# Feed-forward by block products: issuing the B11 + B12 difference behind the splits of the three-block sum

## The chip, the cores and the metric

The kernel runs on one core of a Trainium2 chip. The metric is the device time of one execution in microseconds (us), as the median of three timed runs. A separate execution was profiled; every duration, start and wait below is from that one.

## What is computed

One layer of a hybrid block on 256 tokens of width 2048, in float32. The part that matters here is the gated feed-forward behind the mixer:

```python
h2 = rms_norm(x, g_ffn)
gate, up = jnp.split(h2 @ w_ffn_in, 2, axis=-1)
x = x + (jax.nn.silu(gate) * up) @ w_ffn_out
```

`w_ffn_in` is 2048 x 11264 and `w_ffn_out` 5632 x 2048.

## The kernel before

**Precision.** TensorE multiplies in fp32r. A weight tile is therefore split in two: ScalarE casts it to `hi` (`whi`, L733), VectorE subtracts to get `lo = w - hi` (`wlo`, L734), and a product is three passes: hi by hi, hi by the lo part of the activations, lo by hi. TensorE can start on a piece when its `whi` is there, and needs its `wlo` after two thirds of the piece (12 matmuls: eight with `whi`, then four with `wlo`).

**The first feed-forward product** is done by groups. There are 22; each has 2 x 128 columns of gate and up, and its 2 x 2 blocks B11, B12, B21, B22 stand in four raw tiles of 128 x 2048. Groups 0 and 1 are multiplied plainly. Groups 2 to 21 use seven block products in place of eight; some of their weights are sums of blocks, and these are made in place:

- B12 + B22: a GpSimd transfer that adds into the tile `x` (L769).
- the three-block sum: `q2` on VectorE, `x = x + b11` (L877).
- B11 + B12: `q1` on VectorE, `b11 = x - b22` (L891).
- the sum with B21: `q4`, a GpSimd transfer that adds `x` into the tile `b21` (L888).

**A cycle** is one group's worth of work. Its products, in the order of the code, are (two pieces each): the next group's pair is already prepared ahead, then C with `x`; B with the three-block sum, whose pieces are called x0 and x1 below; A with `b21` (b21-0, b21-1); B with B11 + B12 (b11-0, b11-1); the next group's first product; B with `b22`; C with the summed `b21`. Between them stand pieces D of the second product (`w_ffn_out`), two in a cycle of groups 3 to 5 and four from group 6 on, and the transposes of the activations.

**Order.** `run` goes through the list of pieces; the split of piece n is written ahead of the products of piece n - 3 (`LOOK = 3`), and each product is followed by what reads its bank. `q2` is written ahead of x0's split and `q1` ahead of b11-0's. A planner then issues, on each engine, the ready instruction that stands first in the code; an instruction written later can be issued earlier when nothing ahead of it is ready. There are four `whi` and four `wlo` buffers, so splits run at most four pieces ahead of TensorE.

The steps that the prediction speaks of on VectorE are, beside L734, L877 and L891: L956 (adds a D piece's result to the residual), L881, L895, L897, L900, L904 (banks read), L805 (gating), L933 (the lo part of the transposed activations; its hi part is L932 on ScalarE).

Of the kernel before, what the change touches and what calls it, by code (L numbers as in the profile page):

```python
# [7 lines left out]
F32 = mybir.dt.float32  # L8
# [38 lines left out]
def block_kernel(ctx: ExitStack, tc: tile.TileContext, xT, vec,  # L47
                 wvf, wqk, wxy, wpi, wgate, wri, wpool, wbr, wout, wffi, wffo, out):
    nc = tc.nc
    V, S, G, PE = nc.vector, nc.scalar, nc.gpsimd, nc.tensor  # L50
# [37 lines left out]
    def split(r, a, n, V=V, S=S):  # L88

        hi = hl_p.tile([P, RAW // 2], F32R, name="whi")  # L90
        lo = hl_p.tile([P, RAW // 2], F32R, name="wlo")
        with tc.high_priority(offset=AHEAD):
            S.copy(hi[:, :n], r[:, a:a + n])  # L93
            V.tensor_sub(lo[:, :n], r[:, a:a + n], hi[:, :n].bitcast(F32))  # L94
        return hi, lo
# [207 lines left out]
    def split_w(k):  # L303
        return split(raws[k // 2], k % 2 * W3, W3, Vo, So)
# [14 lines left out]
    for k in range(EARLY):  # L319
# [7 lines left out]
        else:  # L327
            w = split_w(k)
# [13 lines left out]
    w = ahead  # L342
# [12 lines left out]
    for k in range(EARLY, KD):  # L355
# [13 lines left out]
        w = ahead  # L369
# [31 lines left out]
    def scores(h, q, k):  # L401

        sc = aux()
        for t in range(2):
            n = (t + 1) * P
            o = sc[:, off[t]:off[t] + n]
            tq = slice(t * P, (t + 1) * P)
            tl = slice(T + t * P, T + (t + 1) * P)
            PE.matmul(o, lhsT=q[:, tq], rhs=k[:, :n], start=True, stop=False)
            PE.matmul(o, lhsT=q[:, tq], rhs=k[:, T:T + n], start=False, stop=False)  # L410
            PE.matmul(o, lhsT=q[:, tl], rhs=k[:, :n], start=False, stop=False)
            PE.matmul(o, lhsT=LF[:, h, tq], rhs=RF[:, h, :n], start=False, stop=True)
        ns = at_p.tile([P, 3 * P], F32, name="ns")
        st = at_p.tile([P, 8], F32, name="st")
        ph = at_p.tile([P, 3 * P], F32R, name="ph")
        pl = at_p.tile([P, 3 * P], F32R, name="pl")
        for t in range(2):
            c = slice(off[t], off[t] + (t + 1) * P)
            V.tensor_tensor_reduce(out=ns[:, c], in0=sc[:, c], in1=mask[:, c], scale=-1.0,
                                   scalar=3e38, op0=ALU.add, op1=ALU.min, accum_out=st[:, t:t + 1])  # L420
            S.activation(ns[:, c], ns[:, c], AF.Exp, bias=st[:, t:t + 1], scale=-1.0,
                         accum_out=st[:, 2 + t:3 + t])
        V.reciprocal(st[:, 4:6], st[:, 2:4])
        for t in range(2):
            c = slice(off[t], off[t] + (t + 1) * P)
            S.activation(ph[:, c], ns[:, c], AF.Copy, scale=st[:, 4 + t:5 + t])
            V.scalar_tensor_tensor(pl[:, c], ns[:, c], st[:, 4 + t:5 + t], ph[:, c].bitcast(F32),
                                   ALU.mult, ALU.subtract)
        return ph, pl
# [47 lines left out]
    for h in range(H):  # L477
# [3 lines left out]
        p = scores(h, q, k)  # L481
# [157 lines left out]
    for m in range(KD):  # L639
# [3 lines left out]
        for b, y in enumerate((yB, yC, yA)):  # L643
            hi, lo = split(r3, b * 1024, 1024) if b < 2 else split(r1, 0, 1024)
# [70 lines left out]
    line, todo = [], []  # L715

    def fill():

        while raws and todo:
            w = todo.pop(0)  # L720
            w.tile = raws.pop(0)
            w.load(w.tile)

    def split_piece(p, ahead):
        for f in p.pre:
            f()
        hi = hl_p.tile([P, RAW // 2], F32R, name="whi")[:, :1024]
        lo = hl_p.tile([P, RAW // 2], F32R, name="wlo")[:, :1024]
        w = p.src()
        if len(w.shape) == 3:  # L730
            hi, lo = halves(hi), halves(lo)
        with tc.high_priority(offset=ahead):
            S.copy(hi, w)  # L733
            V.tensor_sub(lo, w, hi.bitcast(F32))  # L734
        for f in p.done:
            f()
        for w in p.uses:
            w.uses -= 1
            if not w.uses:
                raws.append(w.tile)  # L740
        fill()
        p.parts = hi, lo
# [12 lines left out]
    def halves(r):  # L755
        return r.rearrange("p (j c) -> p j c", j=2)
# [28 lines left out]
    def product(g, w, form, c, start, pre=None, done=None, post=None, more=()):  # L785

        for h in range(2):
            def mm(hi, lo, h=h):
                o = g.place(c)
                for part, v in ((0, hi), (1, hi), (0, lo)):  # L790
                    for j in range(4):
                        PE.matmul(o, lhsT=hs[:, 4 * h + j, form, part, :], rhs=v[:, :, j * P:(j + 1) * P],  # L792
                                  start=start and h == 0 and part == 0 and v is hi and j == 0,
                                  stop=h == 1 and v is lo and j == 3, skip_group_check=True)

            Piece(lambda h=h: halves(w.tile)[:, :, h * 512:(h + 1) * 512], mm, [w, *more],
                  [pre] if pre and h == 0 else [], [done] if done and h else [],
                  [post] if post and h else [])

    def tmp(nm):  # L800
        return ft_p.tile([P, T], F32, name=nm)

    def gated(t, a, up, g):

        V.scalar_tensor_tensor(a, up, r2[:, t:t + 1], g, ALU.mult, ALU.mult)  # L805
# [4 lines left out]
    def first(g):  # L810
        if g.i in PLAIN:
            both(g, g.b11, (("C", 4, True), ("A", 0, True)), lambda: less(g, "t0", "A", "C"))
        else:
            product(g, g.b11, 0, "A", True, post=lambda: copy(g, "m1", "A"))
# [59 lines left out]
    def group(g, nxt, slot, mid):  # L874

        def q2():
            V.tensor_add(g.x.tile, g.x.tile, g.b11.tile)  # L877

        def d():
            g.d = sm.tile([P, T], F32, name="t0")  # L880
            V.tensor_sub(g.d, g.m1, g.bank["B"])  # L881

        def silu0():
            g.g0 = sm.tile([P, T], F32, name="t1")
            S.activation(g.g0, g.bank["A"], AF.Silu, scale=r2[:, 0:1])

        def q4():
            G.dma_start(g.b21.tile, g.x.tile, accum_op=ALU.add)  # L888

        def q1():  # L890
            V.tensor_sub(g.b11.tile, g.x.tile, g.b22.tile)  # L891

        def s():
            s_ = sm.tile([P, T], F32, name="evt")
            V.tensor_sub(s_, g.bank["B"], g.m1)  # L895
            g.u1 = tmp("u1")
            V.tensor_sub(g.u1, s_, g.bank["C"])  # L897

        def up0():
            V.tensor_sub(g.m1, g.bank["B"], g.m1)  # L900
            gated(0, g.m1, g.m1, g.g0)

        def end():
            V.tensor_add(g.d, g.d, g.bank["C"])  # L904
            S.activation(g.d, g.d, AF.Silu, scale=r2[:, 1:2])
            gated(1, g.u1, g.u1, g.d)

        product(g, g.x, 4, "C", True)
        slot(0)

        product(g, g.x, 5, "B", True, pre=q2, post=d, more=[g.b11])
        mid()
        product(g, g.b21, 1, "A", False, done=q4, post=silu0, more=[g.x])
        slot(1)
        product(g, g.b11, 3, "B", False, pre=q1, post=s, more=[g.x, g.b22])
        if nxt is not None:
            first(nxt)
        slot(2)
        product(g, g.b22, 6, "B", False, post=up0)
        product(g, g.b21, 2, "C", False, post=end)  # L920
        slot(3)

    def turn(g, c, f):

        if f == 0:
            acts[c] = act_p.tile([P, 2 * max(CHUNKS), 2 * T], F32R, name="act")
        act = acts[c]
        tp = aux_p.tile([P, 2, T], F32, name="turn")
        for j in range(2):
            for t, a in enumerate((g.m1, g.u1)):  # L930
                PE.transpose(tp[:, j, t * P:(t + 1) * P], a[:, j * P:(j + 1) * P], ident.bitcast(F32))  # L931
        S.copy(act[:, f:f + 2, :T], tp)  # L932
        V.tensor_sub(act[:, f:f + 2, T:], tp, act[:, f:f + 2, :T].bitcast(F32))  # L933
# [42 lines left out]
    def behind(f):  # L976

        line[-1].post.append(f)
# [14 lines left out]
    for i, (c, at) in enumerate(owner):  # L993
        g, prev = nxt, (g if i else None)
        nxt = Group(i + 1) if i + 1 < len(owner) else None

        def slot(k):
            if nxt is None and k == 3:
                return
            for _ in range(SLOTS[c][k]):  # L1000
                if queue:
                    queue.pop(0)()

        def mid():
            if prev is None:
                behind(stats)
                return
            pc, pat = owner[i - 1]
            behind(lambda a=(prev, pc, 2 * pat): turn(*a))
            if pc != c:  # L1010
                queue.extend(down(pc))

        (plain if i in PLAIN else group)(g, nxt, slot, mid)
# [145 lines left out]
```

## Time and profile before

| | |
|---|---|
| median of three timed runs | 1528.62 us (1528.33 to 1530.21) |
| the profiled execution's own time | 1532.99 us |
| its span, first to last instruction | 1531.0 us |
| TensorE matmul busy | 1508.2 us, 99% |
| TensorE weight loads busy | 1411.3 us, 92% |
| VectorE busy | 1205.4 us, 79% |
| ScalarE busy | 923.8 us, 60% |
| mean granted TensorE clock | 0.997 |

The span begins and ends with the program's instructions; the execution's own time is 1.99 us longer. The shares are means over the whole kernel; the feed-forward begins near 820 us, and there VectorE is busier than 79%.

### The profile page before, as it was taken

The numbers are of one execution on the slowest core, as the hardware profiler recorded it, in microseconds if no ns is written. First come the engines' busy times: TensorE is split into PE (matmuls) and PEld (weight loads), VectorE is DVE, ScalarE is ACT, GpSimd is POOL, SyncE is SP. The second block draws the span as 40 slices with busy tenths as digits, with TensorE's granted clock in tenths as the row PEclk, the third lists the DMA queues.
The fourth block names the chain that finished last, engine by engine and source line by source line (L and its number), as shares of the span: only waits on it lengthen the run. The fifth ranks groups of instructions, "written<-read, shape, count | busy, mean of one in ns | idle before, by whom it ended". The sixth has DMA issues, their size and how long they took to land.

```text
span 1531.0 us, 26475 instructions
## 1 busy us (share of the span) xinstructions
PE 1508.2 (99%) x10628; PEld 1411.3 (92%) x10628; DVE 1205.4 (79%) x1593; ACT 923.8 (60%) x1319; POOL 119.5 (8%) x170
## 2 busy tenths in 40 slices
PE   9999999999999999999999999999999999999996
PEld 8988888888888888888889999999999999999996
DVE  7866677788565656567796999999889998999974
ACT  6766567666454444455675666566565665656663
POOL 1000011202000000000110010010000000000012
PEclk9999999999999999999999999999999999999998
DMA  7644455555555554656757699878889888887851
GB/s 259 212 165 150 135 192 185 200 173 206 189 183 199 172 207 165 206 170 234 264 187 219 197 254 277 286 228 252 258 275 295 243 249 267 281 278 242 238 204 55
DMA packets 70858, 331.09 MB, mean 216 GB/s; under 512 B 5584, under 2 KB 6480, under 8 KB 52816
## 3 DMA queue, kind: packets, MB, share of 16 engines
q1 hardware_dynamic: 61840, 286.54, 52.3%
q0 software_dynamic: 8320, 41.95, 14.5%
q8 instruction: 83, 1.36, 0.3%
q10 hardware_dynamic: 576, 0.92, 0.2%
q14 instruction: 39, 0.32, 0.1%
HBM read 306.32 MB, written 2.10 MB: 201 GB/s over the span
## 4 chain that ended last, share of the span: by engine, by line
PE 90%; DVE 4%; DMA 2%; issue 1%; ACT 1%; POOL 0%; SPq 0%; POOLq 0%; DVEq 0%; ACTq 0%
PE acc L106 30%; PE bank L792 23%; PE acc L107 15%; PE obank L117 5%; PE obank L116 5%; PE obank L115 5%; PE bank L834 3%; DVE wlo L734 2%; DMA raw<-raw 2%; PE acc L72 1%; PE aux L72 1%; PE turn L931 1%; DMA raw<-in_wvf 1%; DVE wlo L72 0%; POOL lev L580 0%
## 5 line engine op out<-in xcount | busy, mean ns | idle before, releaser
L733 ACT CAST whi<-raw 128x1024 fp32r<-128x1024 f32 x384 | 393.9, 1050 | 226.9 <-PE obank L116 57.5
L734 DVE TENSOR_TENSOR wlo<-raw,whi 128x1024 fp32r<-128x1024 f32 x384 | 456.4, 1220 | 61.5 <-ACT whi L733 59.0
L106 PE MATMUL acc<-hT,whi 128*128 128x512 f32 x1392 | 489.7, 395 | 0.0
L94 DVE TENSOR_TENSOR wlo<-raw,whi 128x1024 fp32r<-128x1024 f32 (+1 forms) x262 | 320.2, 1222 | 188.9 <-ACT whi L93 188.2
L93 ACT CAST whi<-raw 128x1024 fp32r<-128x1024 f32 (+1 forms) x262 | 270.2, 1032 | 208.5 <-PE acc L106 181.6
L107 PE MATMUL acc<-hT,wlo 128*128 128x256 f32 x1392 | 390.7, 281 | 0.0
L106 PEld LDWEIGHTS acc<-hT,whi 128*128 128x128 f32 x1392 | 261.6, 188 | 59.4
L792 PE MATMUL bank<-whi,hs 128*128 128x256 f32 x2240 | 312.6, 281 | 1.5 <-ACT whi L733 1.5
L792 PEld LDWEIGHTS bank<-whi,hs 128*128 128x128 f32 x2240 | 284.0, 188 | 2.4 <-ACT whi L733 2.1
L107 PEld LDWEIGHTS acc<-hT,wlo 128*128 128x128 f32 x1392 | 262.4, 189 | 0.0
L115 PE MATMUL obank<-act,whi 128*128 128x256 f32 x704 | 197.5, 281 | 0.0
L116 PE MATMUL obank<-act,whi 128*128 128x256 f32 x704 | 197.4, 280 | 0.0
L117 PE MATMUL obank<-act,wlo 128*128 128x256 f32 x704 | 197.3, 281 | 0.0
L792 PE MATMUL bank<-wlo,hs 128*128 128x256 f32 x1120 | 179.1, 282 | 4.6 <-DVE wlo L734 4.4
L792 PEld LDWEIGHTS bank<-wlo,hs 128*128 128x128 f32 x1120 | 151.9, 188 | 7.1 <-DVE wlo L734 6.7
L116 PEld LDWEIGHTS obank<-act,whi 128*128 128x128 f32 x704 | 132.6, 188 | 0.0
L115 PEld LDWEIGHTS obank<-act,whi 128*128 128x128 f32 x704 | 132.4, 188 | 0.0
L117 PEld LDWEIGHTS obank<-act,wlo 128*128 128x128 f32 x704 | 132.3, 188 | 0.1
L106 PE MATMUL acc<-mT,whi 128*128 128x512 f32 x256 | 89.6, 394 | 0.0
L107 PE MATMUL acc<-mT,wlo 128*128 128x256 f32 x256 | 71.5, 280 | 0.0
L769 POOL DMA_DIRECT2D raw<-in_wffi x20 | 24.2, 1210 | 514.7 <-DVE wlo L734 262.6
L106 PEld LDWEIGHTS acc<-mT,whi 128*128 128x128 f32 x256 | 48.1, 188 | 11.2 <-DVE mT L655 0.2
(288 smaller groups left out, 1766.9 us busy)
## 6 DMA issues: line engine op xcount, KB each, us to landing
raw<-in_wffi SPq DMA_DIRECT2D x88, 1024.0 KB, 7.3
raw<-in_wgate SPq DMA_DIRECT2D x48, 1024.0 KB, 4.9
raw<-in_wffo SPq DMA_DIRECT2D x44, 1024.0 KB, 8.6
raw<-in_wffi POOLq DMA_DIRECT2D x20, 1024.0 KB, 8.3
raw<-raw POOLq DMA_DIRECT2D x20, 1024.0 KB, 11.4
raw<-in_wqk SPq DMA_DIRECT2D x16, 1024.0 KB, 4.8
raw<-in_wxy SPq DMA_DIRECT2D x16, 1024.0 KB, 4.9
raw<-in_wbr SPq DMA_DIRECT2D x16, 1024.0 KB, 5.0
```

Source lines behind the costliest of these rows:

```text
L72: self.last = f(*args, **kw)
L93: S.copy(hi[:, :n], r[:, a:a + n])
L94: V.tensor_sub(lo[:, :n], r[:, a:a + n], hi[:, :n].bitcast(F32))
L106: PE.matmul(ps, lhsT=hi[:, w], rhs=rhs(k), start=first and k == 0, stop=False)
L107: PE.matmul(ps[:, :T], lhsT=lo[:, w], rhs=rhs(k)[:, :T], start=False, stop=last and k == nk - 1)
L115: PE.matmul(o, lhsT=hi[:, w], rhs=rhs(k)[:, :T], start=first and k == 0, stop=False)
L116: PE.matmul(o, lhsT=hi[:, w], rhs=rhs(k)[:, T:], start=False, stop=False)
L117: PE.matmul(o, lhsT=lo[:, w], rhs=rhs(k)[:, :T], start=False, stop=last and k == nk - 1)
L733: S.copy(hi, w)
L734: V.tensor_sub(lo, w, hi.bitcast(F32))
L792: PE.matmul(o, lhsT=hs[:, 4 * h + j, form, part, :], rhs=v[:, :, j * P:(j + 1) * P], start=start and h == 0 and part == 0 and v is hi and ...
L834: PE.matmul(o, lhsT=hs[:, 4 * h + j, form, part, :], rhs=v[:, :, j * P:(j + 1) * P], start=start and h == 0 and part == 0 and v is hi and ...
```

## The change

`q1`, the subtraction that makes B11 + B12, gets an order edge: it may not be issued on VectorE before the second `wlo` split of the three-block sum (x1's) has been issued. The edge orders issue alone; it adds no wait for a result. Nothing else is added or removed, and no instruction changes its operands.

```diff
         with tc.high_priority(offset=ahead):
             S.copy(hi, w)
-            V.tensor_sub(lo, w, hi.bitcast(F32))
+            p.sub = V.tensor_sub(lo, w, hi.bitcast(F32))
...
         def q1():
-            V.tensor_sub(g.b11.tile, g.x.tile, g.b22.tile)
+            with tc.issue_after(g.sums.sub.ins):
+                V.tensor_sub(g.b11.tile, g.x.tile, g.b22.tile)
...
         product(g, g.x, 5, "B", True, pre=q2, post=d, more=[g.b11])
+        g.sums = line[-1]
         mid()
```

## Rows read from the trace of the kernel before

**Rows 1.** Waits of TensorE's weight loads, 980 to 1470 us, then 850 to 980.

```profile
PEld bank L792 <- DVE wlo L734: 6.1, 8, 1.5
...
PEld bank L792 <- ACT whi L733: 2.1, 3, 0.8
PEld bank L792 <- DVE wlo L734: 0.6, 3, 0.2
```

**Rows 2.** Waits of TensorE's matmuls over the whole span: total us, times, longest.

```profile
PE bank L792 <- DVE wlo L734: 4.4, 6, 1.3
```

**Rows 3.** VectorE in order of time, group 10: start, us, instruction, count.

```profile
1088.45 2.28 DVE L877 TENSOR_TENSOR raw<-raw,raw 128x2048 f32<-128x2048 f32 x1
1090.65 0.41 DVE L956 TENSOR_TENSOR xt<-xt,obank 128x256 f32<-128x256 f32 x1
1090.98 2.28 DVE L891 TENSOR_TENSOR raw<-raw 128x2048 f32<-128x2048 f32 x1
1093.19 3.49 DVE L734 TENSOR_TENSOR wlo<-raw,whi 128x1024 fp32r<-128x1024 f32 x3
1096.60 0.41 DVE L956 TENSOR_TENSOR xt<-xt,obank 128x256 f32<-128x256 f32 x1
1096.93 2.35 DVE L734 TENSOR_TENSOR wlo<-raw,whi 128x1024 fp32r<-128x1024 f32 x2
1099.20 0.41 DVE L881 TENSOR_TENSOR t<-m,bank 128x256 f32<-128x256 f32 x1
1099.53 0.68 DVE L933 TENSOR_TENSOR act<-turn,act 128x512 fp32r<-128x512 f32 x1
1100.13 1.22 DVE L734 TENSOR_TENSOR wlo<-raw,whi 128x1024 fp32r<-128x1024 f32 x1
```

**Rows 4.** ScalarE in the same stretch, with the idle time before each.

```profile
1090.85 4.84 ACT L733 CAST whi<-raw 128x1024 fp32r<-128x1024 f32 x5 [3.30 <-DVE raw L877]
1096.17 1.05 ACT L733 CAST whi<-raw 128x1024 fp32r<-128x1024 f32 x1 [0.48 <-PE bank L792]
```

**Rows 5.** TensorE's weight loads in the same stretch: x0, x1 and b11-0.

```profile
1091.95 1.00 PEld L792 LDWEIGHTS bank<-whi,hs 128*128 128x128 f32 x8
1094.46 0.54 PEld L792 LDWEIGHTS bank<-wlo,hs 128*128 128x128 f32 x4 [1.50 <-DVE wlo L734]
1094.92 1.01 PEld L792 LDWEIGHTS bank<-whi,hs 128*128 128x128 f32 x8
1095.86 0.55 PEld L792 LDWEIGHTS bank<-wlo,hs 128*128 128x128 f32 x4
...
1102.47 1.00 PEld L792 LDWEIGHTS bank<-whi,hs 128*128 128x128 f32 x8
```

**Rows 6.** Group 10's transfer q4, and the cast and split that wait for it.

```profile
1098.45 0.90 POOL L888 DMA_DIRECT2D raw<-raw  x1 [1.56 <-DVE wlo L734]
...
1111.40 1.05 ACT L733 CAST whi<-raw 128x1024 fp32r<-128x1024 f32 x1 [3.80 <-DMA raw<-raw]
...
1112.48 1.23 DVE L734 TENSOR_TENSOR wlo<-raw,whi 128x1024 fp32r<-128x1024 f32 x1 [3.33 <-ACT whi L733]
```

**Rows 7.** The same VectorE idle time in groups 14 and 19.

```profile
1239.43 1.22 DVE L734 TENSOR_TENSOR wlo<-raw,whi 128x1024 fp32r<-128x1024 f32 x1 [0.54 <-ACT whi L733]
...
1399.41 1.23 DVE L734 TENSOR_TENSOR wlo<-raw,whi 128x1024 fp32r<-128x1024 f32 x1 [3.80 <-ACT whi L733]
```

**Rows 8.** Cycles: window, length, then busy us (count) of PE, PEld, DVE, ACT, POOL.

```profile
878.28:905.23 26.95, 26.95 (x228) 26.76 (x228) 26.95 (x32) 17.87 (x20) 2.09 (x2) 1.00 0.92 258
905.23:932.30 27.07, 26.64 (x221) 26.07 (x220) 27.04 (x31) 17.93 (x20) 2.09 (x2) 1.00 0.94 273
932.30:959.48 27.18, 26.71 (x223) 26.19 (x222) 27.04 (x32) 17.87 (x20) 2.09 (x2) 1.00 0.94 272
1088.45:1121.09 32.64, 31.34 (x266) 31.14 (x265) 29.31 (x34) 19.72 (x22) 2.10 (x2) 1.00 0.84 253
1214.99:1246.55 31.56, 31.56 (x270) 31.56 (x269) 29.58 (x33) 20.30 (x22) 2.10 (x2) 1.00 0.91 283
```

**Rows 9.** VectorE in order of time in an early cycle, group 4.

```profile
905.23 2.29 DVE L877 TENSOR_TENSOR raw<-raw,raw 128x2048 f32<-128x2048 f32 x1
907.43 0.48 DVE L805 SCALAR_TENSOR_TENSOR u<-u,r,t 128x256 f32<-128x256 f32 x1
907.95 0.42 DVE L956 TENSOR_TENSOR xt<-xt,obank 128x256 f32<-128x256 f32 x1
908.28 2.28 DVE L891 TENSOR_TENSOR raw<-raw,raw 128x2048 f32<-128x2048 f32 x1
```

**Rows 10.** VectorE around b11-0's split in group 13, and TensorE's start on b11-0.

```profile
1195.11 1.22 DVE L734 TENSOR_TENSOR wlo<-raw,whi 128x1024 fp32r<-128x1024 f32 x1
...
1198.20 0.54 PEld L792 LDWEIGHTS bank<-whi,hs 128*128 128x128 f32 x4
```

## The prediction

> **What bounds the kernel now.** I read the page first: TensorE is busy 99% of the span, so a change on VectorE can only win back what TensorE loses by waiting. Next the waits of TensorE, to see how much that is and for whom. In the feed-forward they are few: 980 to 1470 us holds eight waits of the weight loads for a `wlo`, 6.1 us together, and 850 to 980 holds three more of 0.6 and three for a `whi` of 2.1 [rows 1]. That is 8.8 us in all, 0.58% of the span. The matmuls' own waits give less, 4.4 us where the loads give 6.7 [rows 1, 2]. I go by the loads: in group 10 eight loads of x0 begin at 1091.95 and the next four at 1094.46, 2.51 later, where x1 takes 0.94 for the same step [rows 5]; the difference of 1.57 is what the loads' row calls 1.50. The Trainium skill says the same (Perfetto Trace Analysis, Identifying the Most-Contended Engine): matmul busy time is a poor measure of TensorE's headroom and the loads' busy share a good one; by the matmuls the ceiling would be 4.4 + 1.5 = 5.9 us, and this trace sides with the loads.
>
> Then VectorE in order of time beside ScalarE, to see why x0's `wlo` is late. In group 10, `q2` ends at 1090.73, an L956 follows, then `q1` holds VectorE from 1090.98, and x0's `wlo` starts at 1093.19, the instant VectorE is free [rows 3]. ScalarE had x0's `whi` ready at 1090.85 + 1.05 = 1091.90 [rows 4]. So `q1` stands in the way.
>
> Last, whole cycles, for VectorE's room. It differs by stage: 27.04 busy of 27.07 and 27.04 of 27.18 in groups 4 and 5, 26.95 of 26.95 in group 3, but 29.58 of 31.56 in group 14 [rows 8]. In three early cycles VectorE, not TensorE, sets the pace (loads busy 26.07 of 27.07); the fifteen late ones have some 2 us of room each.
>
> **Part 1: `q1` leaves its place.** Without it x0's `wlo` can start 0.04 behind its `whi` (the distance of 1112.45 to 1112.48 elsewhere [rows 6], rounded up), at 1091.94 instead of 1093.19: 1.25 us earlier. Of the 1.50 wait 0.25 stays, and every wait under 1.25 at this place goes. Each of the eight late ones is at x0, the longest 1.5 [rows 1]: at most some 6.1 - 2 x 0.25 = 5.6 back from them by this step alone. The next splits move up with it.
>
> **Part 2: where `q1` goes.** The edge names x1's `wlo`, but the planner decides. VectorE's order behind `q1` is that of the code: x0, x1, b21-0, L956, b21-1, D, L881, L933, b11-0 [rows 3]. Only `q1` stands out of its turn: its place in the code is right in front of b11-0, and it was drawn forward while x0's `whi` was not ready. With the edge there is such a hole behind x1 only if b21-0's `whi` is late, and ScalarE casts five pieces in 4.84 us, 0.95 each [rows 4], against some 1.14 a split (3.49 for three, which overlap by 0.08). So I expect b21-0 first, and `q1` at its written place, behind L933.
>
> **Part 3: what waits for `q1` there.** Behind it on ScalarE's queue stands b11-0's cast, which ran at 1096.17 [rows 4] and must now wait; behind that cast, b11-1's and the next group's. In group 10, `q1` begins at 1100.13 - 1.25 = 1098.88 [rows 3] and ends 2.28 later, 1101.16; the cast starts 0.12 later (as 1090.73 to 1090.85) and is done at 1102.33, 2.20 behind the old start of b11-0's `wlo`. TensorE reached b11-0 at 1102.47 [rows 5], 2.34 behind the same start, but now comes earlier by what it got back at x0, here 1.25. So 1.11 of the 1.25 is lost again. By the same steps every late cycle keeps only 0.14 of its gain: eight cycles, 8 x 0.14 = 1.1 us. This is the lower bound of the late gain. A cycle without a wait has cover: in group 13 the cast is done at 1195.11 + 2.20 = 1197.31, and TensorE arrives at 1198.20 [rows 10].
>
> **Part 4: what else moves up.** `q4` is issued 0.3 behind b21-1's `wlo` (the first of the two at 1096.93, over at 1098.15 [rows 3, 6]). That split runs 1.25 earlier, so the transfer does too. In group 10 its landing is what starts ScalarE again at 1111.40 after 3.80 idle, and VectorE after 3.33 [rows 6]; from there VectorE runs nearly without pause into the next `q2`. VectorE now reaches this point 2.24 later (1102.37 against 1100.13 at b11-0), so of 3.33 idle 1.09 is left for the earlier landing to use: the next cycle starts 1.1 earlier, and that covers a loss of up to 1.1 at its b11-0. The idle time here goes from 0.54 to 3.80 [rows 7], so some cycles gain all and some nothing. Of the 6.1 - 1.1 = 5.0 that part 3 takes back, I let 1.6 stand, nearer to the row of group 10 than to that of group 14, because the long waits come in cycles that follow a long idle time. Late gain: 6.1 - 1.6 = 4.5, between 1.1 and 6.1 (an earlier cycle start also takes the last 0.25 at x0).
>
> **Part 5: the early cycles pay.** The change puts two holes into VectorE's order where none was: between `q2` and x0's `wlo` (0.12 + 1.05 + 0.04 = 1.21) and between `q1` and b11-0's (1.21 again). In groups 3 to 5 VectorE has no idle time, so what is not filled lengthens the cycle. Fillers are there: an L805 (0.40 of spacing) and an L956 (0.33) run between `q2` and `q1` now [rows 9] and leave 0.48 of the first hole; the second can take one or two L956 of the D pieces, 0.33 each, which leaves 0.55 to 0.88. Together 1.0 to 1.4; taking 1.0 for three cycles, 3.0, and 0.1 for group 6, which has some room behind: 3.1. The bounds are 0 (everything filled) and 2 x 1.21 x 4 = 9.7. The 2.7 of waits that these cycles show now [rows 1] is TensorE waiting for a VectorE that is full; it is no separate gain. The page cited above counts VectorE's occupancy as a fair measure of its room, which agrees with 27.04 of 27.07; by that rule every hole left open there is paid in full.
>
> **Sum.** -4.5 + 3.1 = -1.4 us. From the profiled span of 1531.0 that gives 1529.6, and of the execution's 1532.99, 1531.6. That execution is 4.4 above the median of the timed runs; the change acts alike on both, so 1528.62 - 1.4, about **1527.2 us**.
>
> **Rivals.** *Clearly faster, 0.34.* Fillers close most of the early holes (cost 1.0, not 3.1), and the earlier `q4` covers b11-0 everywhere: -6.0 + 1.0 = -5.0, 1523.6. For it: L956 wait nearby in each early cycle, and the long late idle times; against it: the 0.54 of group 14. *Slower by the early holes, 0.12.* In groups 3 to 6 neither hole is filled, 9.7, and the late gain of 4.5 stands: +5.2, 1533.8. It decides from 4.5 / 4 = 1.1 us of open hole a cycle on. Against it: the two fillers of rows 9 are ready at that place. *Slower by `q1` right behind x1, 0.11.* If the planner sees b21-0's `whi` late, `q1` takes the place the edge names. Then VectorE idles 1.21 - 0.33 = 0.88 before x0, and all from b21-0 on comes 0.9 to 1.0 later than now: the old wait moves from x0 to b21-0, D's split is late too, and `q4` is issued 0.9 later, which carries into the next cycle. Some 10 of 19 cycles would pay 0.9: +9, 1537.6. For it: the five casts are only 0.19 a piece ahead of VectorE; against it: they are ahead. *No effect.* That the order stays as it was is excluded in the cycles shown, since `q1` stands ahead of x0 in them; that all cancels is inside the forecast.
>
> **How the numbers follow.** The forecast has 0.43, its own range 1524.5 to 1530.5. A change of 0.2%, 3.1 us, is about what a measurement of this kernel can tell from none: under 1525.6 is faster, above 1531.7 slower. Faster: 0.34 and a little of the forecast, 0.36; slower: 0.12 + 0.11 = 0.23; same: 0.41. The range for 8 in 10 leaves out the far half of each outer case: 1521.5 to 1534.5; its lower end is the late bound of 6.1 with 1.0 more of the early waits, its upper the early bound with a late gain near 3.7.
>
> **What would show it.** Right: behind `q2` on VectorE come x0, x1, b21-0, b21-1; `q1` stands behind L933 or L881; the late waits at x0 are gone; those left are at b11-0 and name L733; b21-0's cast after `q4` starts about 1 us earlier in its cycle; the cycles of groups 3 to 5 grow from 27.1 towards 28. Wrong: `q1` between x1 and b21-0 or b21-1 (the second slower rival); early cycles as long as before (the fast one); early cycles over 28.3 (the first slower one); or waits of TensorE at products that show none now.

## The result, and the profile after

The change makes the kernel slower: 1573.71 us median (1572.59 to 1575.45, four runs) against 1528.47 (1527.01 to 1530.21, four runs); the ratio is 1.028, with an interval of 1.0261 to 1.0299, some 43 us. Forecast were 1527.2 us, and at most 1537.6 by any rival. The profiled span grew by 39.9, from 1531.0 to 1570.9. The granted clock is 0.996 against 0.997, so the clock is not it. Lines 891 to 956 of the kernel before are L892 to L958 now, and the down weights' load L945 is L947.

First the page of the kernel after (busy time, and the chain that ended last):

```profile
PE 1527.6 (97%) x10628; PEld 1416.2 (90%) x10628; DVE 1207.3 (77%) x1593; ACT 911.8 (58%) x1319; POOL 119.5 (8%) x170
...
PE 64%; DVE 18%; DMA 8%; issue 5%; ACT 4%; POOL 0%; SPq 0%; DVEq 0%; ACTq 0%; POOLq 0%
PE acc L106 29%; PE acc L107 15%; DVE wlo L734 9%; PE bank L792 8%; DMA raw<-in_wffo 5%; PE bank L834 3%; ACT whi L733 3%; DVE raw L892 2%; DVE raw L877 2%; DMA raw<-raw 2%; PE obank L116 2%; PE obank L117 2%; PE obank L115 2%; PE acc L72 1%; DMA raw<-in_wvf 1%
```

Two links of the chain are new or have grown: loads of down weights (in_wffo, 5%, not in the list before), and splits (9%, 2% before). No engine has become full; something waits.

Then the cycles, cut at the first weight load of x0 (columns as in [rows 8]): three early ones together and the fourteen from group 7 to group 21. The kernel before:

```profile
882.97:963.49 80.52, 79.63 (x663) 78.33 (x661) 80.24 (x92) 53.00 (x60) 5.07 (x5) 1.00 0.95 273
996.55:1444.83 448.28, 443.75 (x3755) 442.25 (x3754) 410.49 (x449) 279.05 (x308) 29.46 (x28) 1.00 0.86 263
```

The kernel after:

```profile
883.81:968.56 84.75, 80.95 (x664) 78.57 (x663) 81.58 (x91) 52.52 (x61) 5.72 (x6) 1.00 0.90 261
1003.00:1483.03 480.03, 460.62 (x3754) 447.60 (x3753) 412.81 (x449) 269.96 (x309) 29.47 (x28) 1.00 0.81 246
```

The three early cycles grow by 4.23 us, as the prediction feared in kind. The fourteen late ones, which were to gain, grow by 31.75: from 32.02 to 34.29 us each. Of the other 3.9, 1.4 is group 6's cycle, 0.8 lies ahead of group 3 and 1.7 behind x0 of group 21. VectorE's busy time hardly moves there (410.49 and 412.81), so it was not given more work.

Next who waits for what. TensorE's weight loads of the kernel after, 980 to 1500 us, answer to [rows 1]:

```profile
PEld obank L117 <- DVE wlo L734: 13.7, 15, 1.0
PEld bank L792 <- DVE wlo L734: 6.7, 29, 0.3
PEld obank L115 <- ACT whi L733: 6.5, 11, 1.5
PEld bank L792 <- ACT whi L733: 5.9, 11, 1.1
PEld obank L116 <- DVE act L935: 1.5, 3, 0.5
```

The old line (6.1 us in eight waits, the longest 1.5) is now 6.7 us in 29 waits of 0.3 at most: the long waits are gone, the total is not. The 5.9 us for a `whi` are all at b11-0, 1.19 behind the end of `q1`: the wait that part 3 of the prediction expects. The largest new line stands at L117 and another at L115, the products of the D pieces, which showed none. And ScalarE's waits for transfers in the same stretch, the kernel before and then after:

```profile
ACT whi L733 <- DMA raw<-raw: 39.7, 14, 4.3
```

```profile
ACT whi L733 <- DMA raw<-in_wffo: 46.0, 12, 4.9
...
ACT whi L733 <- DMA raw<-raw: 0.9, 2, 0.6
```

Before, the waits were for `q4`'s landing and none was for a down weight. Now ScalarE waits for a down weight that has not come. So the question goes to the queue that loads them: SP, which the prediction never looked at. SP around the end of group 9's cycle, in the kernel before (L945 loads a down weight, L765 a block of the first weight):

```profile
1069.42 0.37 SPq L945 DMA_DIRECT2D raw<-in_wffo  x1
...
1078.68 0.37 SPq L765 DMA_DIRECT2D raw<-in_wffi  x1
1079.14 0.42 SPq L945 DMA_DIRECT2D raw<-in_wffo  x1
1079.66 0.41 SPq L765 DMA_DIRECT2D raw<-in_wffi  x1
```

And after:

```profile
1087.26 0.37 SPq L765 DMA_DIRECT2D raw<-in_wffi  x1
1087.72 0.93 SPq L947 DMA_DIRECT2D raw<-in_wffo  x2
1090.16 0.37 SPq L765 DMA_DIRECT2D raw<-in_wffi  x1
```

Two loads have changed places. When b11-1 is split, two raw tiles come free: that of `b11`, which takes the next down weight, and that of `x`, which takes the next group's `b21` and may be written only when `q4` has read `x`. In the code the down weight's load stands first. The planner keeps that order in the kernel before, and turns it round in the kernel after. The down weight is now issued behind a load that waits for `q4`: in these rows 0.46 us after that load. SP's own waits at that load, over the whole span (total us, times, longest), the kernel before and then after:

```profile
SPq L765 <- DMA raw<-raw: 113.7, 15, 8.9
```

```profile
SPq L765 <- DMA raw<-raw: 285.8, 15, 19.8
```

Fifteen times as before, but SP now comes to the wait early (its last issue ahead of 1087.26 was at 1067.54) and stands there with the down weight behind it. From group 7 on, the traces of the two kernels differ in the order of issue by one move a cycle on three engines, `q1` on VectorE, one cast on ScalarE and this load on SP, and TensorE's order is the same.

### The profile page after: what moved, and what is told of

Same layout as the page of the kernel before. It is cut to its first block, busy times and chain, and to the rows that moved or that the text cites. A ratio compares the mean times of both kernels' runs of the same rounds, so it can differ in the third digit from the quotient of the medians.

```text
span 1570.9 us, 26451 instructions
## 1 busy us (share of the span) xinstructions
PE 1527.6 (97%) x10628; PEld 1416.2 (90%) x10628; DVE 1207.3 (77%) x1593; ACT 911.8 (58%) x1319; POOL 119.5 (8%) x170
## 4 chain that ended last, share of the span: by engine, by line
PE 64%; DVE 18%; DMA 8%; issue 5%; ACT 4%; POOL 0%; SPq 0%; DVEq 0%; ACTq 0%; POOLq 0%
PE acc L106 29%; PE acc L107 15%; DVE wlo L734 9%; PE bank L792 8%; DMA raw<-in_wffo 5%; PE bank L834 3%; ACT whi L733 3%; DVE raw L892 2%; DVE raw L877 2%; DMA raw<-raw 2%; PE obank L116 2%; PE obank L117 2%; PE obank L115 2%; PE acc L72 1%; DMA raw<-in_wvf 1%
## 5 line engine op out<-in xcount | busy, mean ns | idle before, releaser
L733 ACT CAST whi<-raw 128x1024 fp32r<-128x1024 f32 x384 | 379.7, 1046 | 252.0 <-DVE raw L892 70.2
L117 PE MATMUL obank<-act,wlo 128*128 128x256 f32 x704 | 199.9, 284 | 10.7 <-DVE wlo L734 10.7
L115 PE MATMUL obank<-act,whi 128*128 128x256 f32 x704 | 199.4, 283 | 4.3 <-ACT whi L733 4.2
L117 PEld LDWEIGHTS obank<-act,wlo 128*128 128x128 f32 x704 | 133.2, 189 | 13.8 <-DVE wlo L734 13.7
L115 PEld LDWEIGHTS obank<-act,whi 128*128 128x128 f32 x704 | 133.2, 189 | 6.5 <-ACT whi L733 6.5
L769 POOL DMA_DIRECT2D raw<-in_wffi x20 | 24.2, 1211 | 540.7 <-DVE wlo L734 387.5
```

Source lines behind the costliest of these rows:

```text
L115: PE.matmul(o, lhsT=hi[:, w], rhs=rhs(k)[:, :T], start=first and k == 0, stop=False)
L117: PE.matmul(o, lhsT=lo[:, w], rhs=rhs(k)[:, :T], start=False, stop=last and k == nk - 1)
```

## The experiments

e1 and e5 differ from the kernel after, and e2 and e10 from the kernel before, in the order or the queue of the loads alone: by the traces VectorE, ScalarE and TensorE issue what they issued there, in the same order. Each ratio is against runs of the kernel before on the same chip. The last three columns are lengths from the profiled execution, cut as above: three early cycles, group 6's, the fourteen late ones. They hold for one execution each: e3's late cycles, issued in the order of the kernel before, are 1.9 us shorter than its, so a difference of 2 us in the last column shows nothing.

| kernel | ratio to before (interval) | early 3 | group 6 | late 14 |
|---|---|---|---|---|
| before | 1 | 80.52 | 33.06 | 448.28 |
| after | 1.028 (1.0261 to 1.0299) | 84.75 | 34.44 | 480.03 |
| e1 after, loads in the old order | 1.0004 (0.9992 to 1.0016) | 84.60 | 33.63 | 441.67 |
| e2 before, loads in the new order | 1.0264 (1.0244 to 1.0284) | 80.55 | 35.04 | 481.06 |
| e3 edge in groups 2 to 6, old loads | 1.0012 (0.9998 to 1.0026) | 84.60 | 33.64 | 446.36 |
| e4 edge from group 7 on, old loads | 0.9976 (0.9966 to 0.9986) | 80.55 | 33.06 | 443.17 |
| e5 after, `b21`'s load on GpSimd's queue | 1.0006 (0.9995 to 1.0017) | 84.52 | 33.64 | 441.87 |
| e7 `q1` between x1 and b21-0, late | 0.9994 (0.9984 to 1.0004) | 81.15 | 33.11 | 446.38 |
| e8 e4, and early `q1` on GpSimd | 1.0103 (1.0086 to 1.0121) | 94.21 | 34.39 | 442.41 |
| e9 e4's edge, `b21`'s load on GpSimd's queue | 0.9977 (0.9966 to 0.9988) | 80.85 | 33.10 | 443.10 |
| e10 before, `b21`'s load on GpSimd's queue | 0.9979 (0.9970 to 0.9988) | 80.78 | 33.10 | 441.87 |

**e1: the change with the loads put back.** Theory: the loads. Rival: `q1`'s place, since ScalarE's casts behind it wait.

```diff
...
         while raws and todo:
             w = todo.pop(0)
             w.tile = raws.pop(0)
-            w.load(w.tile)
+            with (tc.issue_after(loads[-1].ins) if loads else nullcontext()):
+                loads.append(w.load(w.tile))
...
```

> The changed kernel, with one thing put back: SP issues the loads in the order of the kernel before (every load queued behind the one written ahead of it). VectorE, ScalarE, GpSimd and TensorE keep the changed kernel's order. Load theory: of the 39.9 us that the profiled span grew, 31.8 lie in the fourteen cycles from x0 of group 7 to x0 of group 21 (34.29 us a cycle, 32.02 before), and come from SP, where the load of b21's next tile, which waits for q4's landing, now stands ahead of a down weight's load. Then this run loses only what the early cycles show (4.2 us) less the late gain forecast in part 4 (1.1 to 4.5): 1526 to 1533 us, the cycles from group 7 on back at 32 us or less, and no cast waiting for a load from in_wffo. Place theory: the late cycles are longer because q1, at its new place, holds back the casts and splits behind it on ScalarE and VectorE (whi after q1, 70.2 us of ScalarE idle). Then this run stays at 1560 us or more with cycles above 34.

Measured: 1532.51 us against 1532.19, a ratio of 1.0004. The late cycles of e1:

```profile
1001.73:1443.40 441.67, 441.67 (x3754) 441.67 (x3753) 411.24 (x447) 274.29 (x307) 28.73 (x28) 1.00 0.87 266
```

31.55 us a cycle, and TensorE's loads are busy for all of it. `q1` stands where the change puts it, the casts still wait for it, and TensorE's loads name a `whi` once, for 0.5 us, between 980 and 1500 us. The place theory falls for the late cycles. That SP's order is now that of the kernel before, as written, is seen in the trace.

**e2: the loads alone.** The other half of the square: the kernel before, with only the two loads exchanged in the late cycles.

```diff
...
+            if w.down and len(raws) and todo and not todo[0].down:
+                late = w
+                continue
-            w.load(w.tile)
+            ins = w.load(w.tile)
+            if late is not None:
+                with tc.issue_after(ins.ins):
+                    late.load(late.tile)
+                late = None
...
```

> The kernel before, q1 where it was, with one thing changed: in the late cycles SP issues the load of b21's next tile ahead of the down weight's load, as the changed kernel does. The four other engines keep the order of the kernel before. Load theory: the late cycles grow to some 34.3 us as in the changed kernel, fifteen cycles by 2.27 us: some 34 us, so 1555 to 1568 us, with casts that wait for in_wffo. Place theory: nothing that holds back a split is changed, so 1527 to 1532 us.

Measured: 1571.52 us, 1.0264, 3.5 us above the expected range: 40 of the 43 us without touching `q1`. The D pieces' waits are those of the kernel after (L742 and L743 are the cast and the split here); the largest line is x0's old wait, grown because every cycle is late:

```profile
PEld bank L802 <- DVE wlo L743: 20.4, 14, 1.5
PEld obank L117 <- DVE wlo L743: 12.9, 15, 1.0
PEld obank L115 <- ACT whi L742: 5.4, 6, 1.5
```

**e5: is it the wait on SP, or the two transfers side by side?** The kernel after with its own order of loads; only the load that waits for `q4` leaves SP's queue.

```diff
-                return lambda r: nc.sync.dma_start(halves(r), block(i, s, h))
+                return lambda r: (G if (s, h) == (0, 1) and i >= 6 else nc.sync).dma_start(halves(r), block(i, s, h))
```

> The changed kernel; from group 6 on, the load of b21's tile (the one that waits for q4's landing) is issued by GpSimd, behind q4 on its queue, instead of by SP. The other loads keep the changed kernel's order on SP, and VectorE, ScalarE and TensorE their whole order. Queue theory: what costs 2.27 us a late cycle is that the down weight's load cannot be issued while SP's queue stands at that wait; with the wait on another queue, it goes out when b11's second split is done, some 4 us earlier, and the late cycles come back to 31.5 to 32.2 us: 1529 to 1536 us, the early cost staying. Transfer theory: the two loads crowd each other on the way, whoever issues them, or GpSimd's next three-block sum comes late behind the wait: cycles of 33 us and more, 1550 us or more.

Measured: 1532.23 us, 1.0006, late cycles 31.56. In group 9, b11-1's split ends at 1075.14, and SP issues the down weight 0.03 later:

```profile
1075.17 4.11 SPq L947 DMA_DIRECT2D raw<-in_wffo  x2
```

GpSimd now stands at the wait for `q4`, with nothing urgent behind it (L888 is `q4`, L765 the load):

```profile
1068.25 0.89 POOL L888 DMA_DIRECT2D raw<-raw  x1 [1.43 <-DVE wlo L734]
1080.48 0.72 POOL L765 DMA_DIRECT2D raw<-in_wffi  x1 [11.34 <-DVE wlo L734]
```

(The split named there had long been done; the last was the transfer of `q4`, whose result ScalarE begins to cast at 1080.02.) So the wait in the queue is the cost, not the transfers' company. The Trainium skill (Perfetto Trace Analysis, DMA Instruction — HWDGE (DVE, Sync)) draws the semaphore wait of such a DMA as time of the issuing sequencer; these runs agree: the wait of SP's queue costs 2.3 us a late cycle (34.36 of e2 against 32.02 before) to 2.7 (34.29 after against 31.56 of e5).

**e3 and e4: the edge by stages, loads in the old order.** e1 with the edge only in groups 2 to 6, or only from group 7 on.

```diff
-            with tc.issue_after(g.sums.sub.ins):
+            with (tc.issue_after(g.sums.sub.ins) if g.i >= 7 else nullcontext()):
```

> The edge of the change only in groups 2 to 6, loads in the old order. Both theories: the early cycles pay as they do in the changed kernel (4.2 us over three cycles, and up to 1.4 in the next), the late ones are as before: 1531.5 to 1534.5 us. If the early growth too comes from loads, 1528 to 1530.

> The edge of the change only from group 7 on, loads in the old order. Load theory with part 4 of the prediction: q1 no longer stands ahead of x0's split, the late waits there go, 1.1 to 6.1 us back: 1522.5 to 1527.5 us. If b11-0 takes back all of it: 1527.5 to 1529. Place theory: the late cycles keep the 2.27 us each that they grew by: 1558 us or more.

Measured: e3 1532.96 us, +1.8 us by its ratio (-0.3 to +4.0); its early cycles are those of e1. e4 1527.78, -3.7 us by its ratio (-5.2 to -2.1). As a bare time e4 lies in the range of "b11-0 takes back all of it", but the kernel before read 1532.19 on that chip, so the ratio decides, and it lies in the range of part 4. What the prediction called a gain is one. What it called a price is one by the cycles (84.60 against 80.52); e3's ratio alone is not clear of 1. Added up they give -1.9 us, where e1 has +0.6 (-1.2 to +2.4): about nothing, within the intervals. TensorE's loads in e4, 980 to 1500 us (L735 and L736 are cast and split):

```profile
PEld bank L795 <- DVE wlo L736: 0.8, 3, 0.3
PEld bank L795 <- ACT whi L735: 0.2, 1, 0.2
```

The holes that the early cycles pay for are seen on VectorE in group 4 of e1 (L880 is `q2`, L895 `q1`, L961 the residual's add):

```profile
908.11 2.28 DVE L880 TENSOR_TENSOR raw<-raw,raw 128x2048 f32<-128x2048 f32 x1
...
911.79 0.42 DVE L961 TENSOR_TENSOR xt<-xt,obank 128x256 f32<-128x256 f32 x1 [0.67 <-PE obank L118]
912.13 5.76 DVE L736 TENSOR_TENSOR wlo<-raw,whi 128x1024 fp32r<-128x1024 f32 x5
...
918.74 2.29 DVE L895 TENSOR_TENSOR raw<-raw,raw 128x2048 f32<-128x2048 f32 x1
920.94 0.78 DVE L961 TENSOR_TENSOR xt<-xt,obank 128x256 f32<-128x256 f32 x2
922.19 5.77 DVE L736 TENSOR_TENSOR wlo<-raw,whi 128x1024 fp32r<-128x1024 f32 x5 [0.47 <-ACT whi L735]
```

0.67 + 0.47 = 1.14 us open, where 1.0 to 1.4 was forecast.

**e7: the second slower rival, made to happen.** The old loads, and from group 7 on `q1` written ahead of b21-0's split, which is queued behind it.

```diff
...
-        product(g, g.b21, 1, "A", False, done=q4, post=silu0, more=[g.x])
+        product(g, g.b21, 1, "A", False, pre=q1 if late else None, done=q4, post=silu0, more=[g.x])
+        if late:
+            line[-2].behind = lambda: g.q1
...
```

> The kernel before with q1, from group 7 on, right behind x1's split and ahead of b21-0's: the place that the edge names, taken literally. Loads in the old order, ScalarE, GpSimd and TensorE as before. By the second slower rival of the prediction, 0.9 us in about half of the cycles (the long waits only move from x0 to b21-0, and q4 is issued 0.9 later): 8 of 15, +7, 1533 to 1537 us. By the late gain of part 4 alone (it is enough that q1 leaves x0's split): 1523 to 1527 us, no different from the run with the late edge.

Measured: 1529.72 us, 0.9994 (-2.4 to +0.6 us). Neither expectation: no loss, and a gain like e4's is not shown (the intervals just overlap). The waits left in the late cycles are small and most are at the D pieces (L118 <- `wlo`, 2.4 us in eight waits of up to 0.4). The rival's 0.9 a cycle was not paid.

**e10 and e9: whose gain is it?** e5's one line put into the kernel before (e10) and into e4 without its load order (e9).

> The kernel before, without the edge; from group 6 on b21's tile is loaded from GpSimd's queue. It tells whose gain the late cycles of the runs above are. If it is the edge's (q1 no longer ahead of x0's split), this run keeps the late waits at x0: 1527 to 1530 us. If it is the loads', the late cycles fall to 31.5 here too: 1523 to 1527 us.

> The edge from group 7 on, no load order imposed; from group 6 on b21's tile is loaded from GpSimd's queue. VectorE, ScalarE and TensorE as in the run with the late edge and the old loads. If the loads cost nothing once the wait is off SP's queue, the two agree: the early cycles of the kernel before (26.2, 27.2, 27.1) and late ones at 31.5 to 31.65: 1523 to 1527 us. If the edge's late gain needs the old load order, 1528 or more.

Measured: e10 1527.06 us, 0.9979; e9 1527.34, 0.9977. Both times lie at or between the edges of the ranges expected, so the waits and the cycles decide. With e4 these are three ways to one floor: 31.56, 31.65 and 31.66 us a late cycle. e10 says the most. `q1` still stands ahead of x0's split in every cycle, and from 980 to 1500 us TensorE's weight loads show no wait at all. Its `q4` lands sooner; time from issue to landing (least, median, longest), the kernel before and then e10:

```profile
DMA to landing us min/median/max: 7.7/11.4/13.3
```

```profile
DMA to landing us min/median/max: 7.7/9.4/11.5
```

In the kernel before, GpSimd issued the next `x`'s adding transfer (L769) at 1095.68 and `q4` at 1098.45; in e10 the two of that cycle stand at 1091.11 and 1095.63, since the load that L769 adds to is no longer behind SP's wait. That their overlap is why `q4` was slow was not tried by itself. e10 is also steadier: its twelve timed executions lie between 1526.50 and 1527.60 us, the 23 of the kernel before on the same chip between 1526.97 and 1534.90. At its best the kernel before is within 0.5 us of e10, so what e10 wins, it wins from the kernel's longer executions.

**e8: an attempt at both.** e4, with `q1` of groups 2 to 6 on GpSimd, to empty the full VectorE.

```diff
-                V.tensor_sub(g.b11.tile, g.x.tile, g.b22.tile)
+                (V if g.i >= 7 else G).tensor_sub(g.b11.tile, g.x.tile, g.b22.tile)
```

> The run with the edge from group 7 on and the loads in the old order, and in groups 2 to 6 q1 computed by GpSimd instead of VectorE, which is full there (27.04 of 27.07 us). If GpSimd is in time for b11-0's cast, three cycles fall from 27.1 towards the 26.1 of the weight loads: 1521 to 1524 us. GpSimd's adds of 128x256 take 1068 ns and of 128x512 1293: a 128x2048 takes between 5.2 and 8.5 us, and b11-0's cast started 5.5 us behind q2 in group 10; so the rival is that the cast waits up to 3 us and q4, behind q1 on GpSimd, up to 1: 1527 to 1540 us.

Measured: 1547.05 us, 1.0103, worse than either forecast. The early cycles take 31.4 us instead of 26.8. GpSimd needs 5.05 us for `q1`, just under the estimate of 5.2 to 8.5, but x0's split, which starts 0.10 behind it, takes 6.04 us instead of 1.22, and TensorE's load waits 3.99 (the first two fences are VectorE and TensorE, the third GpSimd):

```profile
884.60 6.04 DVE L736 TENSOR_TENSOR wlo<-raw,whi 128x1024 fp32r<-128x1024 f32 x1 [0.80 <-ACT whi L735]
```

```profile
890.70 0.93 PEld L795 LDWEIGHTS bank<-wlo,hs 128*128 128x128 f32 x4 [3.99 <-DVE wlo L736]
```

```profile
884.50 5.05 POOL L895 TENSOR_TENSOR raw<-raw,raw 128x2048 f32<-128x2048 f32 x1
```

## Why the prediction was wrong, step by step

**The step that failed is part 2, "where `q1` goes": "Only `q1` stands out of its turn."** It asked what the planner does with VectorE's order and took the order of every other queue as it was, so a change on SP stands in the sum at nothing, without a reason. The runs put some 40 us on it (e2). On VectorE part 2 was right. Group 9 of the kernel after:

```profile
1067.82 2.29 DVE L877 TENSOR_TENSOR raw<-raw,raw 128x2048 f32<-128x2048 f32 x1
1070.03 0.42 DVE L958 TENSOR_TENSOR xt<-xt,obank 128x256 f32<-128x256 f32 x1
1071.30 3.50 DVE L734 TENSOR_TENSOR wlo<-raw,whi 128x1024 fp32r<-128x1024 f32 x3 [0.86 <-ACT whi L733]
1074.72 0.41 DVE L958 TENSOR_TENSOR xt<-xt,obank 128x256 f32<-128x256 f32 x1
1075.05 2.35 DVE L734 TENSOR_TENSOR wlo<-raw,whi 128x1024 fp32r<-128x1024 f32 x2
1077.32 0.42 DVE L881 TENSOR_TENSOR t<-m,bank 128x256 f32<-128x256 f32 x1
1077.65 2.29 DVE L892 TENSOR_TENSOR raw<-raw 128x2048 f32<-128x2048 f32 x1
```

x0, x1, b21-0, an L958, b21-1, D, then `q1` behind L881: the order forecast, with `q1` one place earlier. But an edge on one engine gave the planner other ready times, and it exchanged two loads on SP. A probable reason, argued only: the tile of `b11` is free when b11-1 is split, and that now comes after a later `q1`, while the tile of `x` waits for `q1` and `q4`; the planner counts the latter as ready first. On the chip it is not: b11-1's split ended at 1083.47 and `q4` landed some 3.8 us later.

What that costs can be followed through group 9 of the kernel after, as a ring in which each step waits for the one before. `q4` is issued at 1076.57. SP passes its wait at 1087.26 and issues the down weight at 1087.72, 4.25 behind the end of b11-1's split, where the kernel before issued it 0.03 behind (1069.42 after 1069.39). ScalarE has been idle for 3.78 when it starts the cast:

```profile
1094.86 3.89 ACT L733 CAST whi<-raw 128x1024 fp32r<-128x1024 f32 x4 [3.78 <-DMA raw<-in_wffo]
```

VectorE, idle for 3.20, then runs without a pause into the next `q2`:

```profile
1095.94 1.23 DVE L734 TENSOR_TENSOR wlo<-raw,whi 128x1024 fp32r<-128x1024 f32 x1 [3.20 <-ACT whi L733]
...
1101.94 2.28 DVE L877 TENSOR_TENSOR raw<-raw,raw 128x2048 f32<-128x2048 f32 x1
```

From `q2` to `q4` is 1076.57 - 1067.82 = 8.75. So this cycle is 8.75 + 10.69 (`q4` to SP's release) + 0.46 + 7.14 (the down weight's load) + 7.08 (its cast to `q2`) = 34.12 us, longer than the 31.55 us that e1's cycles take with TensorE's loads busy throughout. In the kernel before the ring was cut: the down weight did not wait for `q4`. e2 closes it with nothing else changed, e1 and e5 cut it in two ways, and the time follows each time.

**The other steps**, read from the kernels without the exchange:

- *What bounds the kernel.* Held. TensorE's waits, 8.8 us, were the ceiling; e4, e9 and e10 win 3 to 4 us by their ratios and leave at most 1.0 us of waits in the late cycles. But the 8.8 were read from one execution, 4.4 us above the median, and "the change acts alike on both" was not shown: the kernel before spreads over 7.9 us, as e10 shows, and another execution need not hold the same waits.
- *Part 1.* x0's `wlo` now follows its `whi` and the long waits are gone, but "`q1` stands in the way" was half of it. In e10 `q1` stands there still, with no wait: so it cost time only in cycles that were late already. That the late `q4` made them late is what e10 suggests; the link was not tried alone.
- *Parts 3 and 4.* The late gain was set at 4.5 us, between 1.1 and 6.1; e4 measures 3.7 (2.1 to 5.2). b11-0's cast does wait for `q1` (in the kernel after TensorE waits for it eleven times), but in e1 TensorE's loads waited for a `whi` only once in the late stretch, so the lower bound, in which each cycle keeps 0.14, was too low.
- *Part 5.* Forecast 3.1 us (0 to 9.7); e1's early cycles are 4.08 longer and group 6's 0.57, 4.65 together. Two of the cycles pay the 1.0 taken, the first 2.0 and group 6's 0.6 instead of 0.1.
- *Sum.* -1.4 us forecast; e1, the change without the exchange, is at +0.6 (-1.2 to +2.4). The late gain came out 0.8 us smaller than forecast and the early price 1.5 larger, so the sum of what was counted was some 2 us off; what was left out weighed some thirty times as much as the sum.
- *The rivals.* None of them has SP's queue in it. The last of the signs named as wrong, waits of TensorE at products that showed none, is the one that came.

## What to carry to other kernels

An ordering edge on one engine is an input to a planner that orders all of them: compare every queue's order before and after, the DMA queues first, before counting what the edge saves. A load that must wait for another transfer holds up all that stands behind it on its queue; give it a queue on which nothing urgent follows, as e5 does with one line; there the same exchange cost nothing that could be measured. Before an instruction is blamed for a wait, look at what made that cycle late: here the same microseconds came back without moving `q1`.

## What the runs showed of the hardware that was not expected

GpSimd's subtraction holds VectorE's up whole, not by a share. In e8 the split starts at 884.60 and ends at 890.64, 1.09 behind the end of GpSimd's subtraction (884.50 + 5.05 = 889.55): about one split's length, as if it had begun only then. All four splits of e8 that start while GpSimd subtracts end 1.08 or 1.09 behind it, and one that was already running when GpSimd began took its usual 1.23 us. The Trainium skill (SBUF — State Buffer, Who interferes with whom) says that a VectorE instruction with two inputs in SBUF and a GpSimd instruction that reads SBUF exclude each other, and the later one waits for the whole of the earlier; this trace agrees where VectorE is the later. The other case it does not show.

And a pause of TensorE was paid twice here. After the wait of 3.99 us in e8, its granted clock is 0.50, the lower level of 1.2 GHz, until about 896.5 us (columns: window, length, busy us and count, clock, DMA share, GB/s):

```profile
891.00:894.00 3.00, 3.00 (x15) 0.50 0.11 21
894.00:897.00 3.00, 3.00 (x17) 0.57 0.21 44
897.00:900.00 3.00, 3.00 (x27) 1.00 1.03 208
```

15 and 17 loads where 27 fit at the full clock: 22 fewer, by estimate some 2.4 us more on top of the 4. The waits of 0.3 to 1.5 us of the kernel after brought no such drop; its late cycles show a clock of 1.00.
